# Products of the delta-rule states in four column strips of the matmul array

## The chip, the cores and the metric

The kernel runs on one core of a Trainium2 chip. The metric is the time of one execution on the device in microseconds (us); the time of a kernel is the median of its runs. One execution is also recorded by the hardware profiler, which lists what each engine did: PE (matmuls; PEld is its loading of weights), DVE, ACT and POOL (element-wise engines), SP (which here issues most transfers), and the DMA engines.

## The reference, cut to what matters

One layer of a decoder trunk is computed for a prompt of 1024 tokens and for 8 decoded samples of one token each. For every sample b and each of 8 heads a state S of 128 x 128 is carried in; the step for one token is

```python
def step(S, inp):
    q_t, k_t, v_t, b_t, g_t = inp
    S = S * jnp.exp(g_t)[..., None, None]
    delta = (v_t - jnp.einsum('bhk,bhkv->bhv', k_t, S)) * b_t[..., None]
    S = S + jnp.einsum('bhk,bhv->bhkv', k_t, delta)
    return S, jnp.einsum('bhk,bhkv->bhv', q_t, S)
```

The kernel needs two products of each of the 64 old states for this, k S and q S: the delta follows from the first, and the output from the second with the scalar product of q and k. Output and new states are results; the output also goes, normed and gated, through the projection w_gdn_out together with that of the prompt. All is in float32.

## The kernel before, in words

The layer is done in stages: modulation and first norm, attention of the prompt, the delta rule of the prompt head by head (with the projections of the next head beside it), then `branches`, then the output projection and the feed-forward part (`second_half`). A float32 matmul of the large projections is made of three matmuls of rounded high and low parts (`mm3`, lines 178 to 180); a weight is loaded into `raw` (L133), and ACT writes its high part (L127), DVE its low part (L128).

`branches` projects the attention's output with w_swa_out in column tiles j = 0 to 7, each over three parts t of the tokens (384, 384 and 264 columns), 24 matmuls a part. One raw buffer and two buffers of high and low parts are there for these weights. DVE multiplies each result with a gate loaded into `sgx` (L1282, loads L1328).

The step of the samples, `sample_delta`, is a generator. `branches` takes one step of it ahead of each part (j, t) from the third part of tile 0 on, and ties its instructions behind the last matmul emitted. So its work is spread between the parts of the projection: loading the states S0 (eight loads L1105, each with the eight samples of a head), norms of q and k, their scalar product, the state products of heads 0 to 3 (L1147, a step), those of heads 4 to 7 (a step), the transposes of the results (through the helper's L188), the delta (L1155 to L1158), its way through DRAM and back as a broadcast (`dlr`, L1165 and L1186), the norm of the output (L1173, L1197, the power on POOL L123, L1200, L1206), and the update of the states (POOL L1187, DVE L1189, store L1191).

For the state products `wide` holds, for head h and sample b, 16 columns: zero but for k in column 2b and q in column 2b + 1. It is the stationary operand, the state the moving one, and the eight samples of a head accumulate into 16 rows of PSUM, so that row 2b is k S and row 2b + 1 is q S of sample b. Before, four heads stand behind each other along the columns of one bank, `ps[16, 4, 128]`; one ACT copy (L1148) brings them to `rows`, and eight transposes of 16 x 128 bring the results to `pks` with the value index on the partitions.

The modulation at the beginning (`modulation`, L262) is of the form that the change takes up: four matmuls with 32 columns of weights write partitions 32j to 32j + 31 of one bank.

The order of the instructions on each engine is not written out: the tile framework plans it with a simulated timeline (`schedule_with_timeline_sim=True`), from priorities (the program order, shifted where streams are woven) and dependencies. PE, DVE, ACT, POOL and SP each take their instructions in the order so planned.

Of the kernel before, what the change touches and what calls it, by code (L numbers as in the profile page):

```python
# [18 lines left out]
P = 128  # L19
NP = 1024  # L20
NS = 8
NT = NP + NS
KC = 8
H = 8
# [22 lines left out]
def carver(*rooms):  # L47

    used = [0] * len(rooms)

    def small(*shape, r=0):
        n = 1
        for x in shape:
            n *= x
        v = rooms[r][:, used[r]:used[r] + n]
        used[r] += n
        letters = "abcd"[:len(shape)]
        return v.rearrange(f"p ({' '.join(letters)}) -> p {' '.join(letters)}", **dict(zip(letters, shape)))

    return small  # L60


class Step:
# [1031 lines left out]
    def sample_delta(self):  # L1095

        nc, I = self.nc, self.I
        zl, cw = self.zl, self.cw
        a, b, c, d, e = (self.t(self.b1, [P, KC, PARTS[t][1]], f"b1{x}{t}", F32R).bitcast(F32).rearrange("p k n -> p (k n)")
                         for x, t in (("h", 1), ("l", 1), ("h", 2), ("l", 2), ("h", 0)))  # L1100
        small = carver(d, e)
        S0 = []
# [15 lines left out]
        wide = small(H, NS, 2 * NS)  # L1118
        nc.gpsimd.memset(wide, 0.0)
        yield  # L1120
        ps = self.t(self.psm, [P, 1], "mm")
        nc.tensor.matmul(ps, flat(sq), self.ones[:, 0:1], start=True, stop=True)
        r = self.rows_rsqrt(small, ps, P, 1.0, 4 * EPS)
# [15 lines left out]
        eg = self.egb[:, :, 0, :].rearrange("p b h -> p h b")  # L1139
        beta = self.egb[:, :, 1, :].rearrange("p b h -> p h b")  # L1140

        rows = small(H, P, r=1)[:2 * NS]
        for h0 in (0, 4):
            ps = self.t(self.psm, [2 * NS, 4, P], "mm")
            for h in range(4):
                for b in range(NS):
                    nc.tensor.matmul(ps[:, h, :], wide[:, h0 + h, b, :], S0[h0 + h][:, b, :], start=b == 0, stop=b == NS - 1)  # L1147
            nc.scalar.copy(rows[:, h0:h0 + 4, :], ps)  # L1148
            yield
        pks = self.t(self.psm, [P, H, NS, 2], "mm")  # L1150
        for h in range(H):
            self.transpose(pks[:, h].rearrange("p b a -> p (b a)"), rows[:, h, :])
        yield
        pk, dl, o = small(H, NS, 2), small(H, NS), small(H, NS)
        nc.vector.tensor_tensor(pk, pks, bc(eg, 3, 2), op=ALU.mult)  # L1155
# [4 lines left out]
        ps = self.t(self.psm, [H * NS, P], "mm")  # L1160
# [11 lines left out]
        ps = self.t(self.psm, [H * NS, 1], "mm")  # L1172
        nc.tensor.matmul(ps, f3(pr), self.ones[:, 0:1], start=True, stop=True)  # L1173
        r = self.rows_rsqrt(small, ps, H * NS, 1.0 / P, EPS)
# [802 lines left out]
```

## Time and profile before

| | |
|---|---|
| median of 3 runs | 2173.14 us (2170.6 to 2176.24) |
| profiled execution | 2178.02 us, of which the span from its first to its last instruction 2176.3 us |
| mean granted clock of PE | 0.974 |
| PE / PEld / DVE / ACT / POOL busy | 96% / 90% / 64% / 39% / 24% of the span |
| HBM | 207.29 MB read, 61.07 MB written |

Times in rows of the profile count from the start of the span. A row of the timeline gives start, duration, engine, line and operation, the tiles written and read, and the shapes; merged instructions have a count (x). In square brackets stands how long the engine had been idle before, and what released it. Durations of matmuls in the records overlap; the distance of their starts tells the pace. An engine's busy share says nothing on what binds a given stretch, so the stretches are looked at one by one.

### The profile page before, as it was taken

What the parts mean: (1) busy time and instruction counts of PE and PEld (TensorE: products, weight loads), DVE (VectorE), ACT (ScalarE), POOL (GpSimd) and SP (SyncE); (2) the same over time, 40 slices, a digit from 0 to 9 for tenths busy, and PEclk for the clock granted to TensorE, in tenths of its full rate; (3) what the DMA queues carried; (4) which work ended last, traced back from release to release, by engine and by line L of the source; (5) the groups of instructions that cost most, each with busy time, mean ns of one, the idle gap of its engine ahead of it and who ended that gap; (6) DMA issues with size and microseconds to landing.
All of it is one profiled execution on the core that took longest, in us unless ns stands there. A gap on an engine that the chain in (4) does not pass through costs nothing. (4 is left out here: it accounts for less than half of the span.)

```text
span 2176.3 us, 41336 instructions
## 1 busy us (share of the span) xinstructions
PE 2084.8 (96%) x16309; PEld 1960.8 (90%) x16309; DVE 1394.8 (64%) x2773; ACT 845.2 (39%) x2102; POOL 517.6 (24%) x589
## 2 busy tenths in 40 slices
PE   7998999999899999999999999999999999999998
PEld 4985887899898988998999999898999999989998
DVE  4656667374555756665323665478888788796885
ACT  4655445334234244344322032244343343333542
POOL 1000000021221110111110300003646556574330
PEclk8999998899999999999999999899999999999999
DMA  8256442151332321221317763511333332389862
GB/s 279 80 137 206 147 138 79 40 143 41 84 82 57 77 56 41 62 66 51 89 60 227 222 188 105 173 62 59 111 102 93 108 98 88 130 270 332 273 200 81
DMA packets 298980, 268.68 MB, mean 123 GB/s; under 512 B 60558, under 2 KB 246321, under 8 KB 298770
## 3 DMA queue, kind: packets, MB, share of 16 engines
q1 hardware_dynamic: 293586, 247.22, 37.5%
q0 software_dynamic: 4912, 18.29, 2.3%
q8 instruction: 128, 2.10, 0.4%
q14 instruction: 66, 0.54, 0.1%
q10 hardware_dynamic: 288, 0.52, 0.1%
HBM read 207.29 MB, written 61.07 MB: 123 GB/s over the span
## 5 line engine op out<-in xcount | busy, mean ns | idle before, releaser
L178 PE MATMUL mm<-b1h,wh 128*128 128x384 f32 (+1 forms) x1392 | 458.0, 330 | 4.5 <-ACT z L764 2.1
L180 PE MATMUL mm<-b1h,wl 128*128 128x384 f32 (+1 forms) x1392 | 453.0, 326 | 3.8 <-DVE wl L128 3.8
L179 PE MATMUL mm<-b1l,wh 128*128 128x384 f32 (+1 forms) x1392 | 450.6, 324 | 0.3 <-DVE b1l L128 0.3
L178 PEld LDWEIGHTS mm<-b1h,wh 128*128 128x128 f32 x1392 | 264.1, 190 | 14.8 <-issue 4.7
L180 PEld LDWEIGHTS mm<-b1h,wl 128*128 128x128 f32 x1392 | 263.9, 190 | 10.3 <-issue 5.5
L179 PEld LDWEIGHTS mm<-b1l,wh 128*128 128x128 f32 x1392 | 264.5, 190 | 3.6 <-issue 1.9
L127 ACT ACTIVATE wh<-raw 128x1024 fp32r<-128x1024 f32 x75 | 78.6, 1048 | 154.5 <-PE mm L179 77.6
L128 DVE TENSOR_TENSOR wl<-raw,wh 128x1024 fp32r<-128x1024 f32 x74 | 92.0, 1243 | 63.9 <-ACT wh L127 63.2
L178 PE MATMUL mm<-pk,w 128*128 128x260 f32 (+1 forms) x440 | 125.1, 285 | 3.0 <-ACT bml L1563 2.4
L179 PE MATMUL mm<-pk,w 128*128 128x260 f32 (+1 forms) x440 | 124.9, 284 | 0.8 <-DVE pk L128 0.8
L180 PE MATMUL mm<-pk,w 128*128 128x260 f32 (+1 forms) x440 | 124.7, 284 | 0.0
L178 PE MATMUL mm<-b2h,wh 128*128 128x384 f32 (+1 forms) x384 | 123.2, 322 | 0.4 <-ACT wh L127 0.4
L180 PE MATMUL mm<-b2h,wl 128*128 128x384 f32 (+1 forms) x384 | 122.0, 320 | 1.3 <-DVE wl L128 1.3
L179 PE MATMUL mm<-b2l,wh 128*128 128x384 f32 (+1 forms) x384 | 122.7, 320 | 0.0
L128 DVE TENSOR_TENSOR w<-ws,w 128x512 fp32r<-128x512 f32 x88 | 74.6, 849 | 36.5 <-ACT w L127 36.5
L178 PE MATMUL mm<-bmh,w 128*128 128x260 f32 (+1 forms) x320 | 92.0, 287 | 0.8 <-DVE fa L1640 0.7
L180 PE MATMUL mm<-bmh,w 128*128 128x260 f32 (+1 forms) x320 | 91.8, 287 | 0.0
L1563 ACT COPY bml<-mm 128x256 f32<-128x256 f32 (+1 forms) x132 | 49.1, 373 | 104.1 <-PE mm L180 97.6
L178 PEld LDWEIGHTS mm<-pk,w 128*128 128x128 f32 x440 | 83.3, 189 | 3.8 <-ACT bml L1563 3.0
L179 PEld LDWEIGHTS mm<-pk,w 128*128 128x128 f32 x440 | 83.4, 190 | 1.0 <-DVE pk L128 1.0
L180 PEld LDWEIGHTS mm<-pk,w 128*128 128x128 f32 x440 | 83.6, 190 | 0.0
L1618 DVE SCALAR_TENSOR_TENSOR fa<-fz,fcw,fa 128x512 f32<-128x512 f32 x88 | 75.0, 860 | 0.4
(639 smaller groups left out, 6076.6 us busy)
## 6 DMA issues: line engine op xcount, KB each, us to landing
raw<-in_w_in_dram SPq DMA_DIRECT2D x60, 512.0 KB
ws<-in_w_ffn_down_dram SPq DMA_DIRECT2D x55, 256.0 KB
raw<-xd SPq DMA_DIRECT2D x47, 258.0 KB
raw<-in_w_ffn_down_dram SPq DMA_DIRECT2D x47, 256.0 KB
raw<-in_w_ffn_gate_dram SPq DMA_DIRECT2D x22, 512.0 KB
raw<-in_w_ffn_up_dram SPq DMA_DIRECT2D x22, 512.0 KB
qst<-in_w_mod_dram SPq DMA_DIRECT2D x16, 512.0 KB
raw<-in_w_mod_dram SPq DMA_DIRECT2D x16, 512.0 KB
```

The source lines that it names most:

```text
L127: self.nc.scalar.activation(hi, x, AF.Copy)
L128: (eng or self.nc.vector).tensor_tensor(lo, x, hi.bitcast(F32), op=ALU.subtract)
L178: mm(ps, whi, xhi, start=first, stop=False, **kw)
L179: mm(ps, whi, xlo, start=False, stop=False, **kw)
L180: self.last_mm = mm(ps, wlo, xhi, start=False, stop=last, **kw).ins
L1563: nc.scalar.copy(r[p, i], x[p])
L1618: nc.vector.scalar_tensor_tensor(ai[:, c:e], zi[:, j + c:j + e], col(j), ai[:, c:e], op0=ALU.mult, op1=ALU.add)
```

## The change

The products of four heads are written to four strips of 32 partitions in one bank, `ps[32h : 32h + 16]`, with the samples as the outer and the heads as the inner loop, so that neighbouring matmuls go to different column strips of the array. Each strip's 16 rows are copied on their own (DVE and ACT in turn) to the same partitions of `rows`, which is now 128 partitions x 2 x 128 and is cleared on POOL beforehand, as the 16 rows between the strips are read by the transposes too. Two transposes of 128 x 128 replace eight of 16 x 128, and `pks` is a view that takes 16 of each 32 columns.

```diff
-        rows = small(H, P, r=1)[:2 * NS]
-        for h0 in (0, 4):
-            ps = self.t(self.psm, [2 * NS, 4, P], "mm")
+        rows = small(2, P, r=1)
+        nc.gpsimd.memset(rows, 0.0)
+        for i in range(2):
+            ps = self.t(self.psm, [P, P], "mm")
+            for b in range(NS):
+                for h in range(4):
+                    nc.tensor.matmul(ps[32 * h:32 * h + 2 * NS], wide[:, 4 * i + h, b, :], S0[4 * i + h][:, b, :],
+                                     start=b == 0, stop=b == NS - 1)
             for h in range(4):
-                for b in range(NS):
-                    nc.tensor.matmul(ps[:, h, :], wide[:, h0 + h, b, :], S0[h0 + h][:, b, :], start=b == 0, stop=b == NS - 1)
-            nc.scalar.copy(rows[:, h0:h0 + 4, :], ps)
+                at = slice(32 * h, 32 * h + 2 * NS)
+                (nc.scalar.copy if h % 2 else nc.vector.tensor_copy)(rows[at, i, :], ps[at])
             yield
-        pks = self.t(self.psm, [P, H, NS, 2], "mm")
-        for h in range(H):
-            self.transpose(pks[:, h].rearrange("p b a -> p (b a)"), rows[:, h, :])
+        pks = self.t(self.psm, [P, 2 * P], "mm")
+        for i in range(2):
+            self.transpose(pks[:, i * P:(i + 1) * P], rows[:, i, :])
+        pks = pks.rearrange("p (h c) -> p h c", c=32)[:, :, :2 * NS].rearrange("p h (b a) -> p h b a", a=2)
         yield
```

## The prediction

> **What bounds the kernel now.** I read the page first (busy times, the slices, the chain), then the busy time by stretches around the changed lines, then the instructions of that stretch in order of time.
>
> ```profile
> span 2176.3 us, 41336 instructions
> ...
> PE 2084.8 (96%) x16309; PEld 1960.8 (90%) x16309; DVE 1394.8 (64%) x2773; ACT 845.2 (39%) x2102; POOL 517.6 (24%) x589
> ...
> PE   7998999999899999999999999999999999999998
> ...
> PE 20%; DVE 3%; DMA 3%; POOL 1%; issue 1%; ACT 0%; SPq 0%; POOLq 0%; DVEq 0%; ACTq 0%
> ```
>
> PE is busy for 96% of the span, in nearly every slice. The chain of waits accounts for less than a third of the span (its shares add up to 28%), so it cannot say what binds the stretch that is changed. The busy time by stretches can. Its columns are the length, then busy time and count for PE, PEld, DVE, ACT and POOL, then granted clock, DMA share and GB/s.
>
> ```profile
> 1140.00:1174.50 34.50, 34.50 (x223) 34.36 (x221) 14.87 (x28) 11.33 (x18) 4.54 (x6) 1.00 1.03 309
> 1174.50:1193.10 18.60, 18.60 (x154) 16.42 (x153) 4.54 (x8) 2.58 (x3) 0.00 (x0) 1.00 0.41 120
> ...
> 1215.00:1250.00 35.00, 32.17 (x190) 31.57 (x189) 29.61 (x75) 2.12 (x2) 14.71 (x8) 0.95 0.86 255
> ```
>
> The second row is the stretch with the state products. PE has no idle time in it, all other engines are mostly idle, and the DMA engines are at 0.41. The stretch is PE's own. The row before it has the DMA engines full (1.03): something that has to arrive may be late just as PE becomes faster. That matters below.
>
> **The change, part by part.** The products first. Min/median/max in ns:
>
> ```profile
> L1147 PEld LDWEIGHTS mm<-b1h,b1l x80: 92/97/97, 1174.5 to 1192.8; 128*16 128x16 f32 x80
> L1147 PE MATMUL mm<-b1h,b1l x80: 272/273/283, 1174.5 to 1192.9; 128*16 128x128 f32 x80
> ...
> L1147 PE MATMUL mm<-b1l,b1l x48: 272/273/283, 1179.8 to 1189.4; 128*16 128x128 f32 x48
> ```
>
> 128 matmul records stand for 64 products, so one product is two passes. The passes overlap in the records, so their durations cannot be added; the timeline gives what they take together.
>
> ```profile
> 1174.29 0.28 PE L180 MATMUL mm<-b2h,wl 128*128 128x264 f32 x1
> ...
> 1174.50 5.41 PE L1147 MATMUL mm<-b1h,b1l 128*16 128x128 f32 x48
> ...
> 1181.59 0.44 PE L178 MATMUL mm<-b2h,wh 128*128 128x384 f32 x1
> ```
> ```profile
> 1185.53 0.33 PE L179 MATMUL mm<-b2l,wh 128*128 128x384 f32 x1
> ...
> 1185.70 0.34 PE L180 MATMUL mm<-b2h,wl 128*128 128x384 f32 x1
> ...
> 1185.97 3.67 PE L1147 MATMUL mm<-b1l,b1l 128*16 128x128 f32 x32
> ...
> 1193.06 0.19 PEld L178 LDWEIGHTS mm<-b2h,wh 128*128 128x128 f32 x1 [0.21 <-issue]
> 1193.06 0.44 PE L178 MATMUL mm<-b2h,wh 128*128 128x384 f32 x1
> ...
> 1197.16 0.34 PE L180 MATMUL mm<-b2h,wl 128*128 128x384 f32 x1
> ...
> 1197.43 0.67 PE L188 MATMUL mm<-ident,b1h 16*128 16x16 f32 x8
> ...
> 1198.02 0.39 PE L178 MATMUL mm<-b2h,wh 128*128 128x264 f32 x1
> ```
>
> The first group takes from 1174.50 to 1181.59, 7.09 us for 64 passes, 0.111 us a pass; the second from 1185.97 to 1193.06, again 7.09. About 0.2 us of the gap at each end of a group is extra beside ordinary spacing (1174.29 to 1174.50; 0.21 idle before 1193.06), and I keep those.
>
> How four strips run side by side is not to be seen in these rows, but the kernel has the same form elsewhere: the modulation (L262) writes four matmuls into partitions 32j of one bank, in f32, with 512 columns. One set of four at full clock, with transposes just before it:
>
> ```profile
> 278.98 0.63 PE L188 MATMUL pt<-ident,E 128*128 128x128 f32 x4
> ...
> 280.01 0.62 PE L262 MATMUL mm<-wmh,cTr 128*32 128x512 f32 x2
> ...
> 280.03 0.62 PE L262 MATMUL mm<-wml,cTr 128*32 128x512 f32 x2
> ...
> 280.47 0.60 PE L262 MATMUL mm<-wmh,cTr 128*32 128x512 f32 x2
> 280.48 0.60 PE L262 MATMUL mm<-wml,cTr 128*32 128x512 f32 x2
> ```
>
> Four records begin within 0.02 us and the other four 0.46 us later: the first passes of four strips run together, then the second passes. A pass of 512 columns over four strips takes 0.46 us, so one of 128 columns takes an estimated 0.46 / 4 = 0.115 us, close to the 0.111 us that a single strip takes today. A new group has 8 samples x 2 passes = 16 such steps, 1.84 us, instead of 7.09. The bounds: no overlap at all (7.09, nothing gained) and the modulation's rate (1.84). I take 1.84, since the row has the same type, the same loop order and the same place of the output; its 32 columns of weights against 16 here can only be the dearer case.
>
> The Trainium skill ("TensorE: Matmul & The Clock Gate", Part 3, "The mechanism") says matmuls start and end strictly in program order, with no reordering. The rows above do not look like that if the two passes of a product are neighbours in the program; what it would cost is a rival below.
>
> What becomes late next: after the first group PE goes on with the third column tile of w_swa_out, and that weight arrives late.
>
> ```profile
> 1169.93 0.41 SPq L133 DMA_DIRECT2D raw<-in_w_swa_out_dram  x1
> ...
> 1175.82 1.06 ACT L127 ACTIVATE wh<-raw 128x1024 fp32r<-128x1024 f32 x1 [17.46 <-DMA raw<-in_w_swa_out_dram]
> ...
> 1177.05 1.22 DVE L128 TENSOR_TENSOR wl<-raw,wh 128x1024 fp32r<-128x1024 f32 x1
> ```
>
> The high part is there at 1176.88, the low part at 1178.27, and neither depends on PE: the load is queued on SP behind the state loads. The new group would end at about 1174.50 + 1.84 + 0.2 = 1176.5. PE then does the first two matmuls from 1176.9 and waits for the low part; that equals a start at 1178.27 - 2 x 0.17 = 1177.9 (0.17 is 1185.70 - 1185.53). So the first group saves 1181.59 - 1177.9 = 3.7 us, not 5.2. That the weight's split hid behind the long products is over: the cover is worth 1.5 us. The weight after it is asked for when that split is done, at 1178.3; if it takes as long as this one (1169.93 to 1178.27, 8.3 us) it is split by 1186.6. The new second group would end near 1184.4 (1177.9, a part of 24 x 0.17 = 4.1, then 2.2), and another part of 4.1 us uses the old weight, so the next is in time. The second group saves 7.09 - 1.84 = 5.2 us, of which I give 0.2 back for unknown tails: 5.0.
>
> The transposes: from 1197.16 to 1198.02 is 0.86 us, less 0.17 for the matmul itself leaves 0.69 for eight. Two of 128x128 take (0.63 - 0.27) / 3 = 0.12 us each by the four at 278.98 (0.27 is what one record lasts), 0.24 plus perhaps 0.15 of change-over: 0.3 saved.
>
> The evictions and the clearing:
>
> ```profile
> 1183.45 0.56 ACT L1148 COPY b1h<-mm 16x512 f32<-16x512 f32 x1
> ```
> ```profile
> 1205.87 0.27 DVE L1163 COPY b1h<-mm 64x128 f32<-64x128 f32 x1
> ```
> ```profile
> 1152.18 0.95 POOL L1119 MEMSET b1l<- 128x1024 f32 x1
> ```
>
> Two ACT copies become four on ACT and four on DVE, each at most 0.56 (ACT) and about 0.27 (DVE): per group 1.1 us of ACT and 0.5 of DVE beside each other. They are behind the products and 4 us ahead of the transposes, which come after another part of the projection: they cost nothing, hidden by those matmuls. Without that cover they would cost 1.1 us. One risk is that DVE's copies stand ahead of the low split of the weight in its queue; the split cannot begin before 1176.88 anyway, so at most 0.5 us. The memset of 256 columns is below 0.95 us on POOL, which does nothing in the whole stretch (0.00 in the second row by stretches). No DMA is added or moved, and no queue passed. The product read after the transposes has the same elements; its cost does not change. With the samples as the outer loop all four states are needed at the first pass; today the fourth (b1l) is first used at 1179.8. The code issues it on SP ahead of the weight load of 1169.93, which had landed by 1175.82, so the group could at worst start 1.3 us late, and that falls into the wait for the weight.
>
> The sum: 3.7 + 5.0 + 0.3 = 9.0 us. What follows (the transposed delta, its trip through DRAM, the update of the states) starts from these products and moves forward with them, and after the stretch PE is busy again in all slices, so the 9.0 should reach the end. The profiled execution took 2178.0; the sum makes it 2169.0. The runs' median is 2173.1, 0.2% below the profiled one: scaled, 2164.2. About 0.3% (6.5 us) is what a measurement of this kernel can tell from no change, so the forecast lies not far outside that.
>
> **The rivals.** *The clock.* PE would now idle 1.4 to 1.8 us in one place. The trace has a like case:
>
> ```profile
> 1223.84 0.43 PE L1206 MATMUL mm<-b1h,ones 64*128 64x64 f32 x2 [1.84 <-DVE b1h L1200]
> ```
> ```profile
> 1224.00:1226.00 2.00, 2.00 (x14) 1.93 (x15) 2.00 (x8) 0.00 (x0) 0.00 (x0) 0.80 0.87 210
> 1226.00:1228.00 2.00, 2.00 (x10) 2.00 (x10) 1.08 (x4) 0.00 (x0) 0.60 (x1) 0.50 1.06 322
> 1228.00:1230.00 2.00, 2.00 (x12) 2.00 (x11) 0.66 (x3) 0.97 (x1) 1.30 (x1) 0.84 1.14 380
> ```
>
> After 1.84 us of idling the granted clock fell to 0.50 for a while. The three rows of 2 us lack 0.20, 0.50 and 0.16 of full clock, 1.7 us of work in all. With that cost 7.3 us are saved, 2165.8. For it: the idle time is of the same kind. Against: it is shorter. 0.10.
>
> *Strict order.* If passes start in program order and a product's two passes are neighbours, only a second pass and the next strip's first can overlap: 4 steps for four strips instead of 2, so 3.7 us a group. The first group would end near 1178.4 (3.2 saved), the second saves 3.4, the transposes 0.3: 6.9, time 2166.2. This is what the skill's sentence comes to here. Against it: the four simultaneous starts above. 0.06.
>
> *It does not do what it says*: strips are taken one after another, 7.1 us a group as today. Only the transposes gain: 2172.8. Against it the same rows; for it only that 16 columns is not the 32 seen there. 0.07.
>
> *The planner.* The order on each engine comes from a simulated timeline, and shorter, or differently priced, products change it for everything behind. A single bad place costs what L1206 costs now, 1.84 idle plus an estimated 1.7 of slow clock, 3.5 us; with two such 2 us of saving are left: 2171. A good one removes that very wait: 2160.7. 0.19 for the first, 0.04 for the second.
>
> *Slower: DVE takes the diagonal of the output norm (L1200) behind the state updates.* PE waits for it in order (L1206 above), and it already comes late:
>
> ```profile
> 1216.45 0.60 POOL L123 TENSOR_TENSOR b1h<-b1h,mhalf 64x1 f32<-64x1 f32 x1
> ```
> ```profile
> 1223.55 0.23 DVE L1200 TENSOR_SCALAR b1h<-ident,b1h 64x64 f32<-64x64 f32 x1
> ...
> 1224.44 2.17 DVE L1189 SCALAR_TENSOR_TENSOR b1h<-b1h,egb,b1l 128x128 f32<-128x128 f32 x8
> ...
> 1248.40 2.19 DVE L1189 SCALAR_TENSOR_TENSOR b1h<-b1h,egb,b1l 128x128 f32<-128x128 f32 x8 [1.80 <-POOL b1l L1187]
> ```
>
> Behind all eight heads it would come at 1250.6 instead of 1223.6, 27 us of waiting against 9 saved: 18 slower, 2191. It turns slower once more than 9 us of updates are added ahead of it, so that it comes after 1232.6 on today's clock. For it: DVE is busy for 29.61 of the 35 us after 1215 (row by stretches), and L1200 already comes 6.5 us after the power that it needs (1216.45 + 0.60). Against: in the code it stands ahead of all state updates. 0.09 with whatever other reordering ends this way. The remaining 0.45 is the forecast.
>
> **How the numbers follow.** Faster by over 0.3%: forecast 0.45, half of the clock case 0.05, half of strict order 0.03, the good order 0.04, and a part of the planner's bad order that costs only one small wait 0.04, together 0.61. Within 0.3%: the other halves 0.08, no overlap 0.07, the rest of the planner's 0.15: 0.30. Slower: 0.09. The range runs from the full gain of 5.2 + 5.2 + 0.3 = 10.7 with the runs' spread (2170.6 to 2176.2 around 2173.1) below it, 2160, to no gain with most of that spread above, 2175.5; it leaves out the slower rival and the extreme of the good order. Within it the forecast's own range is 2161 to 2168.
>
> **What would show it.** In the changed profile, records of the product line should begin in fours within 0.05 us, and each group should last 1.8 to 2.2 us; at 3.7 strict order holds, at 7 nothing overlaps. The first L180 after the first group should wait for the low split by 1 to 2 us. Two transposes of 128x128 should stand where eight stood. The part behind, up to the oa loads, should be the old one 9 us earlier with the same waits, L1206's 1.84 among them. Wrong would be: groups as long as before, new PE waits on DVE or DMA beyond 1193 that add up to more than 3 us, or a clock below 1.00 near the new wait.

## The result, and the profile after

| | before | after |
|---|---|---|
| median | 2173.47 us (12 runs) | 2161.49 us (12 runs) |
| ratio to before | | 0.9945, interval 0.9931 to 0.996 |
| the same once more, on another occasion (29 and 12 runs) | 2172.06 us | 2160.86 us, ratio 0.9953, 0.9933 to 0.9972 |

The kernel became 10 to 12 us faster; 9.0 had been forecast. The page of the kernel after:

```profile
span 2155.9 us, 41331 instructions
...
PE 2065.6 (96%) x16303; PEld 1944.9 (90%) x16303; DVE 1390.5 (65%) x2777; ACT 846.5 (39%) x2104; POOL 522.9 (24%) x590
```

The two profiled spans differ by 20 us, far more than the medians. They cannot be subtracted. The first state product starts at 1174.50 before and at 1167.47 after, although PE's work ahead of it is the same in both (8664 matmul records each): 7 us of the 20 lie where nothing was changed. In a second profile of the changed kernel it starts at 1172.80. So I count from the first state product on, up to the start of the fourth column tile of w_swa_out (busy time by stretches, columns as in the prediction; before, then after):

```profile
1174.50:1201.04 26.54, 26.54 (x210) 24.08 (x210) 6.56 (x15) 3.16 (x4) 0.00 (x0) 1.00 0.32 92
```
```profile
1167.47:1184.27 16.80, 15.86 (x204) 14.76 (x203) 7.16 (x17) 3.15 (x6) 0.00 (x0) 1.00 0.50 146
```

The same work takes 26.54 us before and 16.80 after: 9.74 us less. The clock is 1.00 in both. After, PE is idle for 0.94 us of it, before for none. PE's timeline of the first group after the change shows the pace, and that wait:

```profile
1167.25 0.28 PE L180 MATMUL mm<-b2h,wl 128*128 128x264 f32 x1
1167.47 0.30 PE L1148 MATMUL mm<-b1h,b1l 128*16 128x128 f32 x3
1167.49 0.28 PE L1148 MATMUL mm<-b1l,b1l 128*16 128x128 f32 x1
1167.59 0.28 PE L1148 MATMUL mm<-b1h,b1l 128*16 128x128 f32 x3
1167.61 0.27 PE L1148 MATMUL mm<-b1l,b1l 128*16 128x128 f32 x1
...
1169.13 0.27 PE L1148 MATMUL mm<-b1l,b1l 128*16 128x128 f32 x1
1169.56 0.44 PE L178 MATMUL mm<-b2h,wh 128*128 128x384 f32 x1 [0.16 <-ACT wh L127]
1169.85 0.34 PE L179 MATMUL mm<-b2l,wh 128*128 128x384 f32 x1
1170.96 0.44 PE L180 MATMUL mm<-b2h,wl 128*128 128x384 f32 x1 [0.78 <-DVE wl L128]
```

Three records from heads 0 to 2 (b1h) and one from head 3 (b1l) begin within 0.02 us, and the next four 0.11 us later. Four strips together advance at the pace that one strip had before. Then PE waits, 0.16 us for the weight's high part and 0.78 for its low part:

```profile
1168.45 1.06 ACT L127 ACTIVATE wh<-raw 128x1024 fp32r<-128x1024 f32 x1 [17.03 <-DMA raw<-in_w_swa_out_dram]
```
```profile
1169.69 1.22 DVE L128 TENSOR_TENSOR wl<-raw,wh 128x1024 fp32r<-128x1024 f32 x1
```

The second group has no such wait; from its first start to the next matmul of the projection are 1.87 us, instead of 7.09:

```profile
1175.00 0.29 PE L1148 MATMUL mm<-b1l,b1l 128*16 128x128 f32 x2
1175.01 0.29 PE L1148 MATMUL mm<-b1h,b1l 128*16 128x128 f32 x2
...
1176.66 0.28 PE L1148 MATMUL mm<-b1h,b1l 128*16 128x128 f32 x2
1176.87 0.44 PE L178 MATMUL mm<-b2h,wh 128*128 128x384 f32 x1
```

And the transposes stand between ordinary matmuls, without a gap around them:

```profile
1180.96 0.34 PE L180 MATMUL mm<-b2h,wl 128*128 128x384 f32 x1
1181.14 0.27 PE L188 MATMUL mm<-ident,b1h 128*128 128x128 f32 x1
1181.17 0.37 PE L178 MATMUL mm<-b2h,wh 128*128 128x264 f32 x1
1181.37 0.28 PE L179 MATMUL mm<-b2l,wh 128*128 128x264 f32 x1
1181.50 0.27 PE L188 MATMUL mm<-ident,b1h 128*128 128x128 f32 x1
1181.52 0.37 PE L180 MATMUL mm<-b2h,wl 128*128 128x264 f32 x1
...
1184.27 0.34 PE L178 MATMUL mm<-b2h,wh 128*128 128x384 f32 x1
```

From that L180 to the fourth tile are 3.31 us; before, from 1197.16 to 1201.04, it was 3.88. The fourth tile before:

```profile
1201.04 0.34 PE L178 MATMUL mm<-b2h,wh 128*128 128x384 f32 x1
```

### The profile page after: what moved, and what is told of

Same layout as the page of the kernel before. It is cut to its first block, busy times and chain, and to the rows that moved or that the text cites. A ratio compares the mean times of both kernels' runs of the same rounds, so it can differ in the third digit from the quotient of the medians.

```text
span 2155.9 us, 41331 instructions
## 1 busy us (share of the span) xinstructions
PE 2065.6 (96%) x16303; PEld 1944.9 (90%) x16303; DVE 1390.5 (65%) x2777; ACT 846.5 (39%) x2104; POOL 522.9 (24%) x590
## 5 line engine op out<-in xcount | busy, mean ns | idle before, releaser
L180 PE MATMUL mm<-b1h,wl 128*128 128x384 f32 (+1 forms) x1392 | 452.6, 326 | 3.8 <-DVE wl L128 3.8
L180 PEld LDWEIGHTS mm<-b1h,wl 128*128 128x128 f32 x1392 | 263.7, 189 | 10.2 <-issue 5.5
L180 PE MATMUL mm<-pk,w 128*128 128x260 f32 (+1 forms) x440 | 124.4, 283 | 0.0
L180 PE MATMUL mm<-b2h,wl 128*128 128x384 f32 (+1 forms) x384 | 122.0, 320 | 2.0 <-DVE wl L128 2.0
L180 PE MATMUL mm<-bmh,w 128*128 128x260 f32 (+1 forms) x320 | 91.1, 285 | 0.0
L180 PEld LDWEIGHTS mm<-pk,w 128*128 128x128 f32 x440 | 83.2, 189 | 0.0
L178 PEld LDWEIGHTS mm<-b2h,wh 128*128 128x128 f32 x384 | 72.8, 190 | 2.8 <-ACT wh L127 2.2
```

Source lines behind the costliest of these rows:

```text
L178: mm(ps, whi, xhi, start=first, stop=False, **kw)
L180: self.last_mm = mm(ps, wlo, xhi, start=False, stop=last, **kw).ins
```

## The experiments

Since a whole run is uncertain by some us, the main reading of each experiment is the same count as above, from its profile: us from the first state product to the points named. Two profiles of one kernel differ by up to 0.4 us in it.

| kernel | PE goes on after group 1 | group 2, start to PE goes on | fourth tile starts |
|---|---|---|---|
| before | 7.09 | 7.09 | 26.54 |
| after | 2.09 | 1.87 | 16.80 |
| after, second profile | 2.22 | 1.87 | 16.94 |
| heads outer | 5.83 | 5.83 | 23.42 |
| two strips | 3.19 | 3.19 | 18.23 |
| one step (both groups: 3.61) | | | 17.27 |
| one step, transposes apart (both: 3.62) | | | 15.19 |
| later states | 2.43 | 1.88 | 17.08 |
| later states, second profile | 2.01 | 1.87 | 16.67 |
| before, products three times | 21.06 | 21.06 | 54.48 |
| after, products five times | 8.85 | 8.86 | 29.70 |

**The order of the loops.** Is it the strips, or that neighbouring instructions go to different strips?

```diff
-            for b in range(NS):
-                for h in range(4):
+            for h in range(4):
+                for b in range(NS):
                     nc.tensor.matmul(ps[32 * h:32 * h + 2 * NS], wide[:, 4 * i + h, b, :], S0[4 * i + h][:, b, :],
```

> The changed kernel with the two loops swapped: four strips as before, but all eight samples of a head behind each other, so that 16 neighbouring passes go to one strip. Theory A (PE starts matmuls in the order of the program, and only neighbours in different strips overlap): a group lasts 64 x 0.11 = 7.1 us as before the change, the wait for the weight is gone again, and of the gain only the transposes' 0.3 to 0.6 us are left, so about 2173. Theory B (each strip has a queue of its own and PE looks far enough ahead to fill all four): groups of 1.8 to 2 us as in the changed kernel, about 2161.5.

Measured: groups of 5.83 us, 2172.69 us beside 2177.95 of before, ratio 0.9972 (0.9957 to 0.9988). Neither theory holds as written. Most of the gain is gone, as A says, but a group is 1.3 us shorter than 7.1. Where the time goes is seen at the border between head 2 (b1h) and head 3 (b1l), in PE's timeline:

```profile
1182.91 0.28 PE L1148 MATMUL mm<-b1l,b1l 128*16 128x128 f32 x1
1183.01 0.27 PE L1148 MATMUL mm<-b1h,b1l 128*16 128x128 f32 x1
1183.03 0.27 PE L1148 MATMUL mm<-b1l,b1l 128*16 128x128 f32 x1
1183.12 0.27 PE L1148 MATMUL mm<-b1h,b1l 128*16 128x128 f32 x1
1183.14 0.27 PE L1148 MATMUL mm<-b1l,b1l 128*16 128x128 f32 x1
1183.23 0.27 PE L1148 MATMUL mm<-b1h,b1l 128*16 128x128 f32 x1
1183.25 1.58 PE L1148 MATMUL mm<-b1l,b1l 128*16 128x128 f32 x13
```

In the program all passes of head 2 precede those of head 3. The program built from this kernel has PE's matmuls in the order of the loops, one for each product, so it is not the planner that mixed them. Yet head 3 starts at 1182.91, ahead of three passes of head 2. PE does look ahead into another strip, but only some four passes far: three borders a group, 1.26 us saved in all, 0.42 a border, is 3.8 passes of 0.11. (The other two borders lie within the tile b1h, where the rows do not tell the heads apart; they are taken to be alike.) So for the full gain neighbours must take different strips, and a strict order of starts is refuted: that PE takes its instructions in the planned order, as the kernel's description has it, does not hold for the starts of passes in different strips.

**Two strips.** Heads 0 and 1 over all samples, then 2 and 3.

```diff
-            for b in range(NS):
-                for h in range(4):
+            for g in (0, 2):
+                for b in range(NS):
+                    for h in (g, g + 1):
```

> The changed kernel, but heads 0 and 1 first and then 2 and 3, each pair over the eight samples: two strips are busy at a time. If the pace is that of a strip (0.11 us a pass in each), a group lasts 32 x 0.11 = 3.5 us plus 0.2; if the order of issue alone limits the overlap (a second pass only with the next strip's first), about the same 3.5, so this run measures the pace only; if four strips ran together for another reason than their number (PE ahead of the records), it would stay at 1.8.

Measured: 3.19 us a group (one run, 2168.49 us):

```profile
1178.32 1.62 PE L1149 MATMUL mm<-b1h,b1l 128*16 128x128 f32 x27
...
1180.10 0.27 PE L1149 MATMUL mm<-b1h,b1l 128*16 128x128 f32 x1
1180.10 0.27 PE L1149 MATMUL mm<-b1l,b1l 128*16 128x128 f32 x1
1180.21 0.27 PE L1149 MATMUL mm<-b1h,b1l 128*16 128x128 f32 x1
...
1181.51 0.44 PE L178 MATMUL mm<-b2h,wh 128*128 128x384 f32 x1
```

That is 32 steps of 0.11, plus the 0.11 that a group of 16 steps had over (1.87 - 1.76), less the 0.42 of one border, 3.2 in all. The pace is a strip's own: with two strips as with four, a step takes 0.11 us, and the time goes with the number of passes that a strip gets.

**Both groups in one step.** The `yield` between the two groups is taken away.

```diff
                 (nc.scalar.copy if h % 2 else nc.vector.tensor_copy)(rows[at, i, :], ps[at])
-            yield
+        yield
```

> The changed kernel without the step between the two groups: both stand ahead of the first part of the third column tile. Theory (the weight's late split leaves PE idle for 0.94 us after the first group in the changed kernel's profile): the second group fills that idle time, and one change-over of about 0.2 us goes. From the first product to the first matmul of the fourth tile 16.8 us become 15.5 to 15.9; time about 1 us below the changed kernel's, too little for the timed rounds. Rival (the planner moves the weight's split behind the copies of the results on ACT and DVE): the wait stays, 16.8 or more.

Measured: the wait for the weight is gone, as expected, but the fourth tile starts at 17.27, not 15.5 to 15.9; ratio 0.9963 (0.9945 to 0.9982). A new wait took its place:

```profile
PE mm L188 <- ACT b1h L1152: 1.6, 2, 1.1
```

The transposes moved a step forward with the groups, and now PE comes to them before the copies that they read are done. ACT's order shows why those were late:

```profile
1181.83 1.06 ACT L127 ACTIVATE wh<-raw 128x1024 fp32r<-128x1024 f32 x1 [3.15 <-DMA raw<-in_w_swa_out_dram]
1182.91 0.26 ACT L1152 COPY b1h<-mm 16x128 f32<-16x128 f32 x1
1184.49 0.26 ACT L1152 COPY b1h<-mm 16x128 f32<-16x128 f32 x1 [1.32 <-DVE b1h L1152]
```

A copy stands behind the split of the next weight, for which ACT waits 3.15 us; and each copy on ACT waits for the one on DVE before it. My rival named the split behind the copies; it was the copies behind the split.

**The same, with the transposes a step later.** A second `yield` ahead of the transposes.

> Both groups of products in one step, as in the run before, but the transposes a step later, so that they no longer stand ahead of the copies on ACT and DVE that they need. Theory: the second group fills the wait for the weight and the transposes find their copies done, so the fourth tile starts 15.2 us after the first product (3.6 for both groups, 4.2 for the first part, 7.4 for the rest as in the changed kernel) instead of 16.8 to 16.9. Time about 1.6 us below the changed kernel, ratio 0.9946 beside its 0.9953, which the timed runs cannot tell apart. Rival (the planner moves the copies or the weight's split behind something else again): a new wait of PE, 16.8 or more.

Measured: 15.19, the 15.2 of the theory. PE's timeline has the group, its end and the fourth tile without a wait in between:

```profile
1178.53 0.30 PE L1148 MATMUL mm<-b1h,b1l 128*16 128x128 f32 x3
...
1182.15 0.44 PE L178 MATMUL mm<-b2h,wh 128*128 128x384 f32 x1
...
1193.72 0.34 PE L178 MATMUL mm<-b2h,wh 128*128 128x384 f32 x1
```

The stretch is 1.6 us shorter than in the changed kernel, and 2.1 us shorter than with the transposes in the same step (17.27), of which 1.6 were the waits for the copies; the ratio of 0.9941 (0.992 to 0.9962) agrees with that, but cannot tell it from the changed kernel's.

**The states of heads 4 to 7 later**, so that the weight is queued ahead of them: their loads L1105 are moved into the third step.

> The changed kernel with the states of heads 4 to 7 loaded two steps later, so that the third tile's weight is queued on SP ahead of them. Theory (that weight is late only because the state loads stand ahead of it): its split is done ahead of the first group's end, no wait of PE there, 16.8 us from the first product to the fourth tile become 15.8. Rival: the second group now waits for its own states, by up to 3 us, and it gets slower by that.

Measured: 17.08 to the fourth tile, the wait still there. SP's order shows that the edit did not do what it was for:

```profile
1157.99 2.10 SPq L1127 DMA_DIRECT2D b1l<-in_state_gdn_S_dram  x2
1160.19 3.48 SPq L1127 DMA_DIRECT2D b1h<-in_state_gdn_S_dram  x2
1163.77 1.66 SPq L133 DMA_DIRECT2D raw<-in_w_swa_out_dram  x1
```

The planner still put the last states (L1127) ahead of the weight (L133). So why the weight is late is argued from the queue's order, not shown. The runs gave a ratio of 0.992 (0.9897 to 0.9942, 6 runs), 17 us, which the stretch does not explain. It was run again, beside the changed kernel itself:

> The changed kernel once more, beside the runs after it. By its stretch around the products it is 9.7 us shorter than the kernel before; the rest of the 12 us that its runs showed would be chance of the granted clock. Theory: a ratio near 0.9955 (9.7 us). Rival (something behind the stretch gains another 2 to 4 us each time): 0.994 or below.

> The kernel with the states of heads 4 to 7 loaded later, once more: its profile showed the same stretch as the changed kernel (17.1 against 16.8 us to the fourth tile, the wait for the weight still there), but its runs were 17 us below the kernel before. Theory: that was chance of the clock, and it lies with the changed kernel, near 0.9955. Rival: it is really 5 us faster than the changed kernel for a reason elsewhere, near 0.992 again.

Measured: 0.9953 (0.9933 to 0.9972) and 0.9953 (0.9936 to 0.9969). They are alike; the 17 us did not return. The clocks of the runs fit the theory of chance. In the six runs of 17 us less, the mean granted clock was 0.978, in those of before beside them 0.974. PE is busy nearly all the time, so the span times the clock takes out most of what the clock does: averaged over the runs it was 7.9 us less than before for those six, 7.1 for the changed kernel's second set and 9.0 for the later states' second set, each known to 1 or 2 us.

**Does time of PE in this place reach the end?** The kernel before with its products three times over, the changed kernel with its products five times.

```diff
-            for h in range(4):
+            for h in [0, 1, 2, 3] * 3:
```
```diff
+            for _ in range(5):
-            for b in range(NS):
-                for h in range(4):
+                for b in range(NS):
+                    for h in range(4):
```

> The kernel before with each head's eight products done three times over in the same rows (the result is that of the last time). Two more groups of 7.09 us each, twice: 28.4 us more of PE in this place. Theory (PE's own time in this place goes to the end one to one, since nothing behind it has slack): 28 us slower, ratio 1.013. Rival (a later wait, for DMA or DVE, takes part of it up): clearly less, for half 1.0065.

> The changed kernel with each group done five times over: 4 x 16 steps x 2 groups at 0.11 us a step are 14.1 us more of PE, of which the first 0.94 fall into the wait for the weight, so 13.1 us. Theory (pace of 0.11 us for four strips holds in a longer stream, and PE binds): groups of 8.8 us, time 13 us above the changed kernel, that is about 2 to 3.5 us above the kernel before. Rival (a longer stream of four strips runs slower than a short one, by weight loads or a lower clock, as more of the array works at once): groups clearly above 9 us or a clock below 1.00 in them.

Measured: before x3 2201.44 us beside 2172.06, ratio 1.014 (1.0107 to 1.0172), 30 us (23 to 37) against the 28.4 expected; the stretch grew by 54.48 - 26.54 = 27.9. The rival's half, 1.0065, lies outside. After x5 2175.85 us, ratio 1.0015 (0.9996 to 1.0033), 3.3 us above before; the stretch grew by 29.70 - 16.80 = 12.9 against 13.1 expected, and groups of 8.85 us are five times 1.76 and a little. What is added to PE here comes out at the end about one to one, as far as the spread of the runs can tell, and four strips keep 0.11 us a step in a longer stream.

## Why the prediction was right

- **The bound.** Right: PE binds the stretch, and time put into it or taken from it reaches the end within the spread of the runs (the two kernels with repeated products, and the change itself).
- **The pace.** Right: 0.115 us a step estimated from the modulation, 0.11 measured; 1.84 us estimated for sixteen steps, 1.76 measured, and 1.87 with the group's end.
- **The first group.** Right in kind: PE waits for the third tile's weight, now that the products no longer cover its split. The term was 3.7 us; from 1167.47 to an equivalent start at 1170.96 - 2 x 0.17 = 1170.62 it is 3.15, so 3.9 was saved. In that execution the low part was ready 3.44 us after the first product, where the one before had 3.77. The wait was 0.94 us by the records, not 1.4 to 1.8. What the late weight costs is more than that: without it the group would have saved 5.2, as the second did, so it costs 1.3 us, where 1.5 had been forecast. The kernel with five times the products agrees: its 14.1 us more of PE less 1.3 are 12.8, and its stretch grew by 12.9. (The next group's end, given as 1184.4, adds up to 1184.2; nothing hangs on it.)
- **The second group.** 5.0 forecast, 7.09 - 1.87 = 5.2 measured.
- **The transposes.** 0.3 forecast, 0.57 measured. The eight took 0.69, so the two take 0.12 together between the other matmuls; 0.24 and a change-over of 0.15 had been allowed for them.
- **The sum.** 9.0 forecast, 9.74 in the stretch; all three terms were 0.2 to 0.3 too small. The medians, 12.0 and 11.2 us apart, have intervals (8.7 to 15.0 and 6.1 to 14.6 us) that hold both 9.0 and 9.74; an excess of 2 us beyond the stretch is not shown by any run.
- **Hidden work.** The copies and the clearing cost nothing in the changed kernel, as forecast. They were assumed to run on ACT and DVE beside each other, and they run in turn (last section); the cover hid that too. That it is thin came out in the one-step kernel: without it PE waited 1.6 us for them.
- **The rivals.** The granted clock stayed at 1.00 around the new wait (the row of the stretch). The like case that this rival was priced by is no fixed rule: in the profile of two strips PE waited 2.05 us for the same diagonal,

```profile
1219.55 0.43 PE L1212 MATMUL mm<-b1h,ones 64*128 64x64 f32 x2 [2.05 <-DVE b1h L1206]
```

and the clock stayed at 1.00, while in the ten other profiles of this case waits of 1.70 to 2.32 us there were each followed, at once or within 1.5 us, by 3.4 us at a clock of 0.50. Strict order is refuted twice, by the groups of 1.87 us and by the starts at the border of two heads. Here the sentence of the Trainium skill ("TensorE: Matmul & The Clock Gate", Part 3, "The mechanism"), that matmuls start and end strictly in program order, and the measured starts differ, and the measurement decides. Of the ends nothing is said: in these records they are modelled. The slower rival did not come: the diagonal of the output norm is waited for as before,

```profile
PE mm L1211 <- DVE b1h L1205: 2.0, 1, 2.0
```

where it had been 1.84, and at the seventh tile the changed kernel is 64.76 - 55.14 = 9.62 us ahead by the same count, so nothing was given back up to there. The start of that tile, before and after:

```profile
1239.26 0.34 PE L178 MATMUL mm<-b2h,wh 128*128 128x384 f32 x1
```
```profile
1222.61 0.34 PE L178 MATMUL mm<-b2h,wh 128*128 128x384 f32 x1
```

## What to carry to other kernels

Products with few output rows (here 16) on a bound PE are worth placing in column strips, if neighbouring instructions go to different strips; with the loops the other way round most of it is lost. Price it from another place of the same trace that has the form already, and then look at what the slow stretch had been hiding: here a weight's split, which took 1.3 us from the gain; filling the wait with the other group, with the transposes a step later, won that back in the stretch. When the gain is half a percent, count from the first changed instruction on; whole spans differed by twice the effect.

## What the runs showed that I had not expected

PE starts matmuls of another strip ahead of earlier ones in the program, about four passes far (0.42 us a border of two heads). And copies from one bank into one tile, dealt out to DVE and ACT, did not run beside each other, though they touch different partitions. Each waits for the other engine's copy of the strip before, in DVE's timeline and ACT's of the kernel after:

```profile
1171.63 0.27 DVE L1152 COPY b1h<-mm 16x128 f32<-16x128 f32 x1
1172.23 0.29 DVE L1152 COPY b1h<-mm 16x128 f32<-16x128 f32 x1 [0.33 <-ACT b1h L1152]
```
```profile
1171.94 0.26 ACT L1152 COPY b1h<-mm 16x128 f32<-16x128 f32 x1 [2.42 <-DVE b1h L1152]
```

They start 0.3 us after each other, in turn, so dealing them out gains little over one engine. The program itself asks for this: each of these copies has a wait on a semaphore that the other engine's copy raises. Whether they would run beside each other without that order was not tried.
